# The first FFN of a hybrid transformer layer rewritten in two phases with a seven-product form

## The chip, the cores and the metric

The kernel runs on one core of a Trainium2 chip. The metric is device time in microseconds, from the start to the end of one execution. All arithmetic that matters is float32, which TensorE is fed as pairs of `float32r` tiles: a high part (a cast copy) and a low part (the rest). Each mathematical product term therefore costs three matmuls.

## The reference

One layer over 1024 latent tokens `x` and 256 context tokens `ctx`, model width 1024, FFN width 2816 (22 blocks of 128 columns). Cut to what matters here:

```
mx = modulation(c, ...);  mc = modulation(c_ctx, ...)         # silu(c) @ w_mod, 9 vectors of 1024 each
def pre(h, g, shift, scale):  return rms_norm(h, g) * (1 + scale) + shift
def swiglu(u, wg, wu, wd):    return (silu(u @ wg) * (u @ wu)) @ wd
x   = x   + 0.5 * gate * rms_norm(swiglu(pre(x, ...),   ...))  # first FFN, both streams, same weights
h_c = h_c + 0.5 * gate * rms_norm(swiglu(pre(h_c, ...), ...))
ux, uc = pre(x, ...), pre(h_c, ...)
x = x + post(token_mixer(ux, uc))                              # attention + gated recurrence
x = x + 0.5 * post(swiglu(pre(x)))                             # second FFN, latent tokens only
```

## The kernel before, in words

Tokens stand in three chunks, `CH`: chunks 0 and 1 are 512 latent tokens each, chunk 2 is the 256 context tokens. Activations lie transposed (features on partitions, tokens along the free dimension). `uh[i]`, `ul[i]` hold the high and low part of the scaled input of chunk i. `term` (L102 to L104) issues the three matmuls of one product term, `mm3` a row of terms.

The program is written as straight Python loops for a tile framework. It inserts all waits, gives out buffers of pools (a pool of n buffers makes the n+1st tile wait), and orders each engine's instructions by their place in the program and by `tc.high_priority()` marks. All DMAs of the part at issue are issued from SP's queue. Every weight goes through a staging tile `st` of a pool with three buffers (`stp`, 512 KB each), shared with the modulation weights `w_mod`; ScalarE casts it to the high part (L93) and VectorE subtracts to get the low part (L94), in `load_w`.

The first FFN is the function `ffn`. For a pair of FFN blocks it loads gate, up and down weights, and for each chunk computes gate and up products into PSUM (`gu`, 8 terms each), applies silu and the multiplication, splits the result in high and low part, and goes on at once with the down products (`down`), which VectorE adds into an SBUF accumulator `ys` (L354). So the weights of a block are loaded once for the three chunks, apart from the first block and the last ones. The first block is done chunk by chunk (`block_by_chunk`), the last blocks in an order of chunks that ends with chunk 1 in two halves of 256 tokens, so that its norm can begin early.

`start1` prepares the inputs: sums of squares (`row_norms`), the first two modulation vectors as dot products on VectorE (`mod_first`, L155), and the scaled input (`build_u`) with GpSimd at L457 and L460 and ScalarE at L458 and L459. Modulation vectors 2 to 8 are 56 tasks (`mod_stream`, L155, 512 wide) that are handed out between the products; a task of vectors 2 to 4 has four dot products, one of 5 to 8 has two.

The residual, the two norms and the next input are a generator, `Norms.chain`, advanced by `pump` calls between products. After the first FFN the token mixer begins with key and value projections and filler projections (tiles `qb`, `fb`) of chunks 2 and 0; chunk 1 is needed only after that.

The second FFN, late in the kernel, already has two phases through device memory (`h_d`) and a seven-product form, `winograd`, of gate and up: two FFN blocks of 128 and two chunks of 512 tokens make a 2 by 2 block product, with the 1024 features cut in two halves. Seven products of four terms replace eight. It has no context tokens and no modulation tasks beside it.

Of the kernel before, what the change touches and what calls it, by code (L numbers as in the profile page):

```python
# [19 lines left out]
P = 128  # L20
D = 1024
# [32 lines left out]
def hybrid_block(ctx: ExitStack, tc: tile.TileContext, xT, cc, cols, w_mod, w_gate, w_up, w_down, w_tok, w_col,  # L54
# [26 lines left out]
    f_d = [dram.tile([512, T], F32, name=f"f{i}_d") for i in range(2)]  # L81
    h_d = dram.tile([DFF, SEQ], F32, name="h_d")
# [221 lines left out]
    def ffn(which, chunks, heads, ends, ys, wp, hp, psA, psB, finish, start, pump, tasks=(), before=lambda sub: None):  # L304
        tasks = list(tasks)
        nblk = NF // 2

        slots = [len(tasks), 0, 14 * (nblk - len(ends[0]) - heads[-1][0]) - 4]

        def work():  # L310
            slots[1] += 1
            while slots[0] - len(tasks) < min(slots[0], slots[0] * slots[1] / slots[2]):
                tasks.pop(0)()

        def gu(ws, sub, k_outer=False, pump=None):
            i, c0, n = sub
            cs_ = slice(c0, c0 + n)
            acc = [[psA.tile([P, 512], F32, name="bank")[:, 0:n] for _ in range(2)] for _ in ws]
            if k_outer:
                order = [(j, e, k) for k in range(KT) for j in range(len(ws)) for e in range(2)]  # L320
            else:
                order = [(j, e, k) for j in range(len(ws)) for e in range(2) for k in range(KT)]
            for j, e, k in order:
                w = ws[j][e]
                term(acc[j][e], (w[0][:, k, :], w[1][:, k, :], uh[i][:, k, cs_], ul[i][:, k, cs_]), k == 0, k == KT - 1)
                if k_outer:
                    if j == len(ws) - 1 and e == 1:
                        pump()
                elif k == KT - 1 and pump:
                    for _ in range(n // 256):  # L330
                        pump()
            hs = []
            for pg, pu in acc:
                sl = hp.tile([P, 512], F32, name="sl", bufs=2)[:, 0:n]
                hh, hl = [hp.tile([P, 512], R, name="h")[:, 0:n] if i < 2 else hp.tile([P, 256], R, name="hc", bufs=4)
                          for _ in range(2)]
                with tc.high_priority():
                    act.activation(sl, pg, AF.Silu)
                    dve.tensor_tensor(sl, pu, sl, op=ALU.mult)  # L339
                    act.copy(hh, sl)  # L340
                    dve.tensor_tensor(hl, sl, f32(hh), op=ALU.subtract)
                hs.append((hh, hl))
            return hs

        def down(ws, hs, sub, d, first, urgent=False):
            i, c0, n = sub
            py = psB.tile([P, 512], F32, name="y")[:, 0:n]
            mm3(py, [(w[0][:, d, :], w[1][:, d, :], h[0], h[1]) for w, h in zip(ws, hs)])
            yd = ys[i][:, d, c0:c0 + n]
            with tc.high_priority(None if urgent else 0):  # L350
                if first:
                    act.copy(yd, py)
                else:
                    dve.tensor_tensor(yd, py, yd, op=ALU.add)  # L354

        def gcol(wsrc, f, eng=dve):
            return load_w(wp, wsrc[which, f], KT, eng)

        def row(f):
            return load_w(wp, w_down[which, f], KT)  # L360

        def block(b, todo):
            fs = (2 * b, 2 * b + 1)
            hs = {sub[0]: [] for sub in todo}
            for f in fs:
# [1056 lines left out]
```

## Time and profile before

| | us |
|---|---|
| median of 3 runs | 2764.76 (2763.84 to 2765.48) |
| the profiled execution: its own time | 2770.57 |
| its span | 2768.8 |
| TensorE busy | 2666.1 (96%) |
| VectorE busy | 1713.5 (62%) |
| ScalarE busy | 1091.9 (39%) |
| GpSimd busy | 163.1 (6%) |

The page divides the span into 40 slices of 69.2 us; the first FFN fills the first 15 of them, the second FFN's products and its down phase the last nine or so. A matmul's busy time is modelled, and matmuls overlap, so their cost is read from the distance of their starts, not from their busy time.

### The profile page before, as it was taken

How to read it: one execution, taken by the hardware profiler on the slowest of the kernel's cores; microseconds unless marked ns; L12 is line 12 of the kernel's file. 1: busy time of each engine (PE TensorE's matmuls, PEld its weight loads, DVE VectorE, ACT ScalarE, POOL GpSimd, SP SyncE). 2: the span in 40 equal slices, each digit the busy share in tenths (PEclk: the TensorE clock that was granted, in tenths of full speed). 3: DMA queues.
4: the chain of work that ended last, by engine and by line, in shares of the span. 5: the costliest groups of instructions: out<-in, count | busy, mean ns of one | idle time of the engine just before them, and what ended most of it. 6: DMA issues, size and time to landing. Idle time of an engine off the chain costs nothing.

```text
span 2768.8 us, 37806 instructions
## 1 busy us (share of the span) xinstructions
PE 2666.1 (96%) x14928; PEld 2283.7 (82%) x14928; DVE 1713.5 (62%) x3268; ACT 1091.9 (39%) x1611; POOL 163.1 (6%) x160
## 2 busy tenths in 40 slices
PE   4799999999999989999999999999999999999998
PEld 3588888888888888989998878887887888888897
DVE  7855554354434887566665559944479776664465
ACT  3531111111111444157776676524354433332443
POOL 4610000000000000110000000001100000000000
PEclk9899999999999999999999999999999999999999
DMA  6562223232211343221111144335344322225474
GB/s 226 170 186 77 69 84 106 69 107 69 70 45 62 100 134 125 87 77 37 45 45 51 35 155 130 104 112 186 125 137 136 114 96 88 73 99 181 165 236 156
DMA packets 138129, 302.49 MB, mean 109 GB/s; under 512 B 13920, under 2 KB 53472, under 8 KB 137952
## 3 DMA queue, kind: packets, MB, share of 16 engines
q1 hardware_dynamic: 137952, 300.08, 33.9%
q8 instruction: 117, 1.92, 0.3%
q14 instruction: 60, 0.49, 0.1%
HBM read 248.13 MB, written 51.90 MB: 108 GB/s over the span
## 4 chain that ended last, share of the span: by engine, by line
PE 83%; DVE 8%; ACT 3%; DMA 3%; issue 2%; POOL 0%; SPq 0%; DVEq 0%; ACTq 0%; POOLq 0%
PE bank L103 17%; PE bank L102 17%; PE bank L104 17%; PE y L102 4%; PE y L103 3%; PE y L104 3%; PE fb L103 3%; PE fb L104 3%; PE fb L102 3%; PE S L756 3%; PE bank L772 2%; PE po L785 1%; PE po L786 1%; DMA st<-in_w_down 1%; PE qb L102 1%
## 5 line engine op out<-in xcount | busy, mean ns | idle before, releaser
L102 PE MATMUL bank<-uh,w 128*128 128x512 f32 (+1 forms) x1888 | 682.0, 363 | 23.9 <-ACT uh L459 14.6
L103 PE MATMUL bank<-ul,w 128*128 128x512 f32 (+1 forms) x1888 | 684.6, 363 | 6.6 <-POOL ul L460 6.6
L104 PE MATMUL bank<-uh,w 128*128 128x512 f32 (+1 forms) x1888 | 683.1, 362 | 0.3 <-DVE w L94 0.3
L102 PEld LDWEIGHTS bank<-uh,w 128*128 128x128 f32 x1888 | 358.2, 190 | 80.2 <-ACT uh L459 17.0
L103 PEld LDWEIGHTS bank<-ul,w 128*128 128x128 f32 x1888 | 358.9, 190 | 62.7 <-POOL ul L460 9.7
L104 PEld LDWEIGHTS bank<-uh,w 128*128 128x128 f32 x1888 | 359.4, 190 | 53.3 <-DVE w L94 0.7
L93 ACT CAST w<-st 128x1024 fp32r<-128x1024 f32 x170 | 176.9, 1048 | 457.6 <-PE y L103 250.2
L94 DVE TENSOR_TENSOR w<-st,w 128x1024 fp32r<-128x1024 f32 x164 | 202.1, 1238 | 151.9 <-ACT w L93 143.4
L102 PE MATMUL fb<-uh,w 128*128 128x512 f32 (+1 forms) x576 | 222.1, 386 | 0.3 <-ACT w L93 0.3
L104 PE MATMUL fb<-uh,w 128*128 128x512 f32 (+1 forms) x576 | 220.0, 382 | 0.0
L103 PE MATMUL fb<-ul,w 128*128 128x512 f32 (+1 forms) x576 | 219.1, 380 | 0.0
L354 DVE TENSOR_TENSOR y<-y,y 128x512 f32<-128x512 f32 (+1 forms) x248 | 144.2, 587 | 107.6 <-PE y L104 106.1
L102 PE MATMUL y<-h,w 128*128 128x512 f32 (+1 forms) x368 | 143.3, 391 | 9.3 <-DVE y L354 5.7
L339 DVE TENSOR_TENSOR sl<-bank,sl 128x512 f32<-128x512 f32 (+1 forms) x68 | 39.9, 588 | 179.2 <-PE bank L104 175.0
L103 PE MATMUL y<-h,w 128*128 128x512 f32 (+1 forms) x368 | 142.4, 387 | 0.0
L104 PE MATMUL y<-h,w 128*128 128x512 f32 (+1 forms) x368 | 141.4, 385 | 0.1
L1132 ACT CAST w<-st 128x512 fp32r<-128x512 f32 x126 | 78.1, 621 | 142.2 <-PE bank L104 128.7
L776 DVE TENSOR_TENSOR pl<-bank,ph 128x512 fp32r<-128x512 f32 x160 | 108.2, 684 | 28.2 <-ACT ph L775 28.2
L1133 DVE TENSOR_TENSOR w<-st,w 128x512 fp32r<-128x512 f32 x126 | 86.7, 690 | 62.1 <-ACT w L1132 61.7
L104 PEld LDWEIGHTS fb<-uh,w 128*128 128x128 f32 x576 | 108.3, 188 | 18.6
L102 PEld LDWEIGHTS fb<-uh,w 128*128 128x128 f32 x576 | 108.5, 188 | 18.1 <-ACT w L93 0.5
L103 PEld LDWEIGHTS fb<-ul,w 128*128 128x128 f32 x576 | 108.4, 188 | 17.8
(290 smaller groups left out, 5119.8 us busy)
## 6 DMA issues: line engine op xcount, KB each, us to landing
st<-in_w_down SPq DMA_DIRECT2D x94, 512.0 KB, 3.7
st<-in_w_mod SPq DMA_DIRECT2D x77, 512.0 KB, 3.7
st<-in_w_gate SPq DMA_DIRECT2D x54, 512.0 KB, 3.7
st<-in_w_up SPq DMA_DIRECT2D x54, 512.0 KB, 3.7
st<-in_w_col SPq DMA_DIRECT2D x36, 512.0 KB, 3.7
hst<-h_d SPq DMA_DIRECT2D x22, 512.0 KB, 4.5
h_d<-pc SPq DMA_DIRECT2D x36, 256.0 KB, 2.0
gate_d<-ft SPq DMA_DIRECT2D x32, 256.0 KB, 2.6
```

The source lines that it names most:

```text
L93: act.copy(hi, st)
L94: eng.tensor_tensor(lo, st, f32(hi), op=ALU.subtract)
L102: pe.matmul(ps, lh, rh, start=first, stop=False)
L103: pe.matmul(ps, lh, rl, start=False, stop=False)
L104: pe.matmul(ps, ll, rh, start=False, stop=last)
L339: dve.tensor_tensor(sl, pu, sl, op=ALU.mult)
L354: dve.tensor_tensor(yd, py, yd, op=ALU.add)
L756: pe.matmul(S[:, cs_], qT[:, (s * 2 + t) * P:(s * 2 + t + 1) * P], kT[g][:, cs_], start=(s == 0), stop=(s == 1))
L772: pe.transpose(pt[:, (a * 2 + t) * P:(a * 2 + t + 1) * P], prob[t][:, kt * P:(kt + 1) * P], ident)
L776: dve.tensor_tensor(pl.rearrange("p a q -> p (a q)"), pt, f32(ph).rearrange("p a q -> p (a q)"), op=ALU.subtract)
L1132: act.copy(h, v)
L1133: dve.tensor_tensor(l, v, f32(h), op=ALU.subtract)
```

## The change

The second FFN's seven-product helper is made general (`operands`, `seven`) and used for the first FFN as well. The first FFN becomes two phases. Phase 1 computes gate and up and writes their product to device memory, `h1_d`. The first four blocks go chunk by chunk with plain products (`head1`, which loads the weights anew for each chunk). For the other nine pairs the x tokens go by seven products; the context tokens keep plain products, with the quarters a11, a12, a21, a22 of the same weights, so that eight tiles are split instead of seven (`whole`). Phase 2 reads `h1_d` back and accumulates the 22 down terms of four output blocks in PSUM, for each chunk and each half of the outputs (`half1`), in the order of chunks 0, 2, 1; the down weights are loaded once for each chunk.

In the input scaling, GpSimd's two multiplications and ScalarE's scale are replaced by two fused VectorE operations; the weights of the first block are split on VectorE instead of GpSimd. The context's first two modulation vectors are computed with chunk 2 instead of chunk 1.

```diff
-    def ffn(which, chunks, heads, ends, ys, wp, hp, psA, psB, finish, start, pump, tasks=(), before=lambda sub: None):
...
+    def operands(wp, src, pr, whole):
+        s = []
+        for e in range(2):
+            st = stp.tile([P, 1024], F32, name="st")
+            sp.dma_start(out=st, in_=src[2 * pr + e])
+            s += [st[:, 0:512], st[:, 512:1024]]
+        a11, a12, a21, a22 = s
+        names = ["a11", "a12", "s1", "s2", "s3", "s4", "a21", "a22"] if whole else ["a11", "s1", "s2", "s3", "s4", "a12", "a22"]
+        ws = {k: wp.tile([P, 1024], R, name="w") for k in names}
...
+        sp_("a11", a11)
+        if whole:
+            sp_("a12", a12)
+            sp_("a21", a21)
+        sp_("a22", a22)
+        s1, s3, s2, s4 = a22, a21, a11, a12
+        dve.tensor_tensor(s1, a21, a22, op=ALU.add)
+        sp_("s1", s1)
+        dve.tensor_tensor(s3, a11, a21, op=ALU.subtract)
+        dve.tensor_tensor(s2, s1, a11, op=ALU.subtract)
+        sp_("s2", s2)
+        if not whole:
+            sp_("a12", a12)
+        dve.tensor_tensor(s4, a12, s2, op=ALU.subtract)
+        sp_("s3", s3)
+        sp_("s4", s4)
...
+    def seven(bank, pc, ws, B, post, work=lambda: None, extra=None):
+        def product(w, b):
+            ps = bank()
+            mm3(ps, quarter(ws[w], B[b]))
+            work()
+            return ps
+
+        p1, p5, u2, u3 = (pc.tile([P, 512], F32, name="pc") for _ in range(4))
+        if extra:
+            extra(0, (ws["a11"], ws["a12"]))
+        ps = product("a11", "b11")
+        with tc.high_priority():
+            act.copy(p1, ps)
+        ps = product("s1", "t1")
+        with tc.high_priority():
+            act.copy(p5, ps)
+        add_now(u2, product("s2", "t2"), p1)
+        if extra:
+            add_now(p1, product("a12", "b21"), p1)
+            post(0, 0, p1)
+        add_now(u3, product("s3", "t3"), u2)
+        add_now(u2, u2, p5)
+        add_now(p5, u3, p5)
+        post(1, 1, p5)
+        add_now(u2, product("s4", "b22"), u2)
+        post(0, 1, u2)
+        if extra:
+            extra(1, (ws["a21"], ws["a22"]))
...
+        add_now(u3, product("a22", "t4"), u3)
+        post(1, 0, u3)
...
-                pool.tensor_tensor(u32, ys[i][:, d, :], rows[i], op=ALU.mult)
-                act.activation(u32, u32, AF.Identity, bias=mods[:, 0, d, s:s + 1], scale=gpre[:, 0, d, s:s + 1])
-                act.copy(h, u32)
-                pool.tensor_tensor(ul[i][:, d, :], u32, f32(h), op=ALU.subtract)
+            dve.scalar_tensor_tensor(u32, ys[i][:, d, :], gpre[:, 0, d, s:s + 1], rows[i], op0=ALU.mult, op1=ALU.mult)
+            act.activation(h, u32, AF.Identity, bias=shift)
+            dve.scalar_tensor_tensor(ul[i][:, d, :], u32, shift, f32(h), op0=ALU.add, op1=ALU.subtract)
...
+    start1(0)
+    head1((0, 1), 0, True)
+    start1(1)
+    for f in range(2, 2 * HEAD):
+        head1((f,), 0)
+    start1(2)
+    for f in range(2 * HEAD):
+        head1((f,), 1)
...
+    for k in range(4):
+        t1 = less(parts(1, k), parts(0, k))
+        t2 = less(parts(1, 4 + k), (t1,))
+        t4 = less(parts(0, 4 + k), (t2,))
+        for j, v in enumerate((t1, t2, t4)):
+            split(th[j][:, k], tl[j][:, k], v)
+    for f in range(2 * HEAD):
+        head1((f,), 2)
+    for k in range(4):
+        v = less(parts(1, 4 + k), parts(1, k))
+        split(uh[1][:, k], ul[1][:, k], v)
...
+    ntask, calls, total = len(tasks), [0], 7 * 2 * (NF // 2 - HEAD) - 16
...
+        seven(bank1, pc, operands(w1, w_gate[0], pr, True), B, gate_post, work, ctx_gate)
+        seven(bank1, pc, operands(w1, w_up[0], pr, True), B, up_post, work, ctx_up)
...
+    def load_h1(i, q):
+        o, n = CH[i]
+        st = stp.tile([P, 1024], F32, name="st")[:, 0:2 * n].rearrange("p (a b) -> p a b", a=2)
+        sp.dma_start(out=st, in_=rows_p(h1_d[2 * q * P:(2 * q + 2) * P, o:o + n]))
+        h, l = place(i, q)
+        split(h, l, st)
...
+    def half1(i, g, order, fresh, after=lambda q: None):
+        n = CH[i][1]
+        ps = [bank1()[:, 0:n] for _ in range(4)]
+        for x, q in enumerate(order):
+            if fresh(x):
+                load_h1(i, q)
+            st = stp.tile([P, 1024], F32, name="st").rearrange("p (a b) -> p a b", a=2)
+            sp.dma_start(out=st, in_=w_down[0, 2 * q:2 * q + 2, :, g * 512:(g + 1) * 512].rearrange("f p d -> p f d"))
+            wh, wl = [w1.tile([P, 1024], R, name="w").rearrange("p (a b) -> p a b", a=2) for _ in range(2)]
+            split(wh, wl, st)
+            for d in range(4):
+                cs_ = slice(d * P, (d + 1) * P)
+                for e in range(2):
+                    term(ps[d], (wh[:, e, cs_], wl[:, e, cs_], *hs[q][e]), x + e == 0, x == NF // 2 - 1 and e == 1)
+            after(q)
+            for _ in range(3):
+                nrm.pump()
...
+    for i in (0, 2, 1):
+        half1(i, 0, pairs, lambda x: True)
+        if i == 1:
+            half1(1, 1, pairs[3:] + pairs[:3], lambda x: x >= 8)
+        else:
+            half1(i, 1, pairs, lambda x: False)
+        for c0 in range(0, CH[i][1], 256):
+            nrm.add((i, c0, 256), ys[i], 0, xT, x1T, 1)
```

## Rows read from the trace of the kernel before

**Rows 1.** The page's slices: tenths busy in 40 slices of 69.2 us.

```profile
PE   4799999999999989999999999999999999999998
DVE  7855554354434887566665559944479776664465
DMA  6562223232211343221111144335344322225474
```

**Rows 2.** Stretches: length, then busy us of each engine, PEclk, DMA, GB/s.

```profile
core 0: us, PE busy (x) PEld busy (x) DVE busy (x) ACT busy (x) POOL busy (x), PEclk, DMA share, GB/s
0.00:200.00 200.00, 140.85 (x634) 112.45 (x635) 146.64 (x277) 84.57 (x139) 85.76 (x60) 0.92 0.61 196
200.00:960.00 760.00, 759.90 (x4002) 652.51 (x4001) 374.26 (x754) 130.12 (x194) 0.00 (x0) 1.00 0.25 78
965.00:980.00 15.00, 7.06 (x43) 5.92 (x42) 14.38 (x29) 5.73 (x9) 0.00 (x0) 0.80 0.74 223
980.00:990.00 10.00, 10.00 (x34) 8.14 (x35) 6.27 (x28) 0.00 (x0) 0.00 (x0) 0.62 0.60 190
```

**Rows 3.** PE groups by line and form, first 200 us: busy, mean ns.

```profile
L103 PE MATMUL bank<-ul,w 128*128 128x512 f32 x102 | 45.6, 447 | 6.6 <-POOL ul L460 6.6
...
L103 PE MATMUL bank<-ul,w 128*128 128x256 f32 x48 | 13.5, 281 | 0.0
L102 PE MATMUL y<-h,w 128*128 128x512 f32 x32 | 13.2, 414 | 3.2 <-ACT y L352 1.7 <-ACT w L93 1.5
...
L102 PE MATMUL y<-hc,w 128*128 128x256 f32 x16 | 4.6, 296 | 0.7 <-ACT y L352 0.7
```

**Rows 4.** PE timeline, start and duration: two 512-wide matmuls, two 256-wide ones.

```profile
399.70 0.39 PE L103 MATMUL y<-h,w 128*128 128x512 f32 x1
...
401.96 0.39 PE L104 MATMUL y<-h,w 128*128 128x512 f32 x1
...
2645.07 0.28 PE L102 MATMUL bank<-uh,w 128*128 128x256 f32 x1
...
2647.95 0.28 PE L102 MATMUL bank<-uh,w 128*128 128x256 f32 x1
```

**Rows 5.** Startup timeline: POOL, a DVE operation beside it and alone, first product.

```profile
15.01 6.94 POOL L94 TENSOR_TENSOR w<-st,w 128x1024 fp32r<-128x1024 f32 x3 [13.71 <-ACT w L93]
...
19.71 2.26 DVE L199 TENSOR_TENSOR nw<-nw 128x4 f32<-128x4 f32 x1
...
22.40 0.16 DVE L199 TENSOR_TENSOR nw<-nw 128x4 f32<-128x4 f32 x1
...
33.88 0.80 PE L102 MATMUL bank<-uh,w 128*128 128x512 f32 x1 [8.08 <-ACT uh L459]
```

**Rows 6.** DVE timeline where it is full: start, duration.

```profile
35.11 1.21 DVE L155 SCALAR_TENSOR_TENSOR st<-st,crow 128x1024 f32<-128x1024 f32 x1
...
260.08 0.69 DVE L155 SCALAR_TENSOR_TENSOR st<-st,crow 128x512 f32<-128x512 f32 x1
260.69 0.08 DVE L155 DVE_READ_ACCUMULATOR st<-st,crow 128x1 f32 x1
260.69 0.69 DVE L155 SCALAR_TENSOR_TENSOR st<-st,crow 128x512 f32<-128x512 f32 x1
...
2131.41 0.70 DVE L1143 TENSOR_TENSOR sl<-y,y 128x512 f32<-128x512 f32 x1
2132.02 0.70 DVE L1133 TENSOR_TENSOR tl<-sl,th 128x512 fp32r<-128x512 f32 x1
...
2140.10 2.36 DVE L94 TENSOR_TENSOR w<-st,w 128x1024 fp32r<-128x1024 f32 x2
```

**Rows 7.** Stretches in the second FFN: its products; its down phase, 256 tokens.

```profile
2200.00:2480.00 280.00, 280.00 (x1237) 231.86 (x1236) 195.57 (x296) 95.84 (x162) 0.00 (x0) 1.00 0.27 89
2640.00:2680.00 40.00, 40.00 (x336) 39.99 (x335) 27.87 (x43) 14.32 (x16) 0.00 (x0) 1.00 0.80 258
```

**Rows 8.** The page's DMA issues: count, size, us from issue to landing.

```profile
st<-in_w_mod SPq DMA_DIRECT2D x77, 512.0 KB, 3.7
```

**Rows 9.** DVE groups of the first FFN, modulation tasks: busy, mean ns, idle before.

```profile
L155 DVE SCALAR_TENSOR_TENSOR st<-st,crow 128x512 f32<-128x512 f32 x112 | 73.5, 688 | 26.4 <-DMA st<-in_w_mod 26.3
...
L155 DVE SCALAR_TENSOR_TENSOR sq<-st,crow 128x512 f32<-128x512 f32 x48 | 31.3, 688 | 13.6 <-DMA st<-in_w_mod 13.5
```

**Rows 10.** The stretch behind the first FFN's last matmul.

```profile
1029.00:1080.00 51.00, 50.86 (x359) 47.33 (x358) 45.21 (x146) 23.56 (x47) 2.88 (x8) 1.00 0.46 141
```

More of the change, by code (lines that the diff above doesn't have):

```diff
@@ new lines, in hybrid_block, with stage, next_spare, start1 @@
+    spare = ys[2].rearrange("p a b -> p (a b)").rearrange("p (t d) -> p t d", d=D)
+    turn = [0]
+    def stage():
+        return stp.tile([P, D], F32, name="st")
+    def next_spare():
+        turn[0] += 1
+        return spare[:, turn[0] % 2] if turn[0] % 3 else stage()
+    def start1(i):
+        if i == 0:
+            with tc.high_priority():
+                row_norms(0)
+            def before(d):
+                mod_first(d, 0, next_spare)
+                if d == 4:
+                    fetch(1)
+                if d == 7:
+                    row_norms(1)
+            build_u(0, before)
+            fetch(2)
+            sp.dma_start(out=crow[1], in_=cc[1:2].partition_broadcast(P))
+            act.activation(crow[1], crow[1], AF.Silu)
+        elif i == 1:
+            def before(d):
+                if d == 4:
+                    row_norms(2)
+            build_u(1, before)
+        else:
+            build_u(2, lambda d: mod_first(d, 1, stage))
@@ new lines, in hybrid_block @@
+    sp.dma_start(out=crow[0], in_=cc[0:1].partition_broadcast(P))
+    sp.dma_start(out=col, in_=cols)
+    act.activation(crow[0], crow[0], AF.Silu)
+    fetch(0)
+    start1(0)
[6 more added lines that the diff above has]
+        head1((f,), 1)
+    e_ctx.close()
+    tp = pool_of(p_ctx, "tk1")
+    th = [tp.tile([P, 4, 512], R, name=f"t1h{j}") for j in range(3)]
+    tl = [tp.tile([P, 4, 512], R, name=f"t1l{j}") for j in range(3)]
@@ L417, in hybrid_block @@
+    while tasks:
+        tasks.pop(0)()
+    p_ctx.close()
+    a_ctx.close()
+    np_ = pool_of(n1_ctx, "ffn1n", side="right")
     nrm = Norms(np_, psN, dg='sq')
@@ new lines, in hybrid_block, with place @@
+        ys[i] = pool_of(cm, f"ffn1d{i}", side="right").tile([P, KT, CH[i][1]], F32, name=f"y{i}")
+    sb = pool_of(f1_ctx, "hs1")
+    hsl = [sb.tile([P, 2, 2, 512], R, name=f"hs{j}") for j in range(4)]
+    slots = [(t[:, 0], t[:, 1]) for t in hsl]
+    slots += [(uh[i][:, q:q + 2], ul[i][:, q:q + 2]) for i in (1, 0) for q in range(0, 8, 2)]
+    def place(i, q):
+        if i == 0:
+            return slots[q]
+        if i == 1:
+            return slots[q % 8]
+        h, l = slots[q // 2]
+        c = q % 2 * 256
+        return h[:, :, c:c + 256], l[:, :, c:c + 256]
@@ L1227, in up_post @@
             sp.dma_start(out=h_d[r0:r0 + P, i * 512:(i + 1) * 512], in_=t)
[L1229 to L1230 removed]
+        seven(bank, pc, operands(wp, w_gate[1], pr, False), B, gate_post)
+        seven(bank, pc, operands(wp, w_up[1], pr, False), B, up_post)
     def slot(f):
```

356 lines of the change are left out of this document (127 added, 229 removed).

## The prediction

> **What bounds the kernel now.** I read the page's slices first [rows 1]: TensorE is full from the third slice on, and VectorE's digits in slices 3 to 13, the first FFN, are 3 to 5. So TensorE sets the pace there, and what is gained or lost in the first FFN is a number of matmuls, or time in which TensorE stands. Then I read stretches [rows 2]. From 200 to 960 us TensorE is busy 759.9 of 760 us and VectorE 374. The losses stand at the two ends: in the first 200 us TensorE is busy 141 us, part of it at a lower granted clock (mean 0.92), and between 965 and 980 us it is busy 7 of 15 us, after which the clock is 0.62 for 10 us.
>
> A matmul's cost is the distance of starts [rows 4]: ten 512-wide ones take 2.26 us, so 0.226 each; 24 of the 256-wide ones take 2.88 us, 0.120 each.
>
> How much is lost at the start? The groups of the first 200 us [rows 3], times three lines, are 402 wide and 192 narrow matmuls: 402 x 0.226 + 192 x 0.120 = 114 us of work, so 86 us are lost.
>
> **The matmuls.** Counted from the code, the first FFN has 3024 wide and 1872 narrow matmuls (the last block's chunk 1 runs as halves of 256). Afterwards: plain heads 4 x 2 x 8 x 3 x 2 = 384 wide, products 9 pairs x 2 x 7 x 4 x 3 = 1512, down 1056, together 2952; narrow ones 1056 + 528 = 1584. That is 683.4 + 224.6 = 908.1 us against 667.2 + 190.1 = 857.2 us: **-50.9 us**. No row speaks of another rate: the second FFN's products run at 0.226 with TensorE never idle [rows 7].
>
> **The startup.** GpSimd leaves it. Its operations slow VectorE: L199 on 4 elements takes 2.26 us while GpSimd splits weights and 0.16 us without it [rows 5]. In exchange VectorE takes GpSimd's work, 24 weight splits (the heads load their weights once per chunk), and the operands T1 to T4. Its list up to the first pair, at distances of starts where it is full [rows 6], 0.61 us for 512 and 1.18 for 1024 elements: norms 22 us; 32 dot products of 1.21 with about 0.4 of small operations, 51; fused scaling 27; weight splits 28; gating 6; 56 operations for T1 to T4, 34; first operand set 7. Together 175 us, behind a start at 9 us and some waits that no edit removes: the first pair at about 188 us, as T3 and the last operands may come later than its first product. DMA says nearly the same: x 5.2 MB, w_mod 16.8, weights 12.6, the first pair 2.1, c 1.0, h1 2.6, in all 40.3 MB, takes 206 us at the 196 GB/s of the first 200 us [rows 2] and 156 us at 258 GB/s, the most that a row shows [rows 7]. TensorE's work until then is 384 x 0.226 + 192 x 0.120 = 110 us, so 78 us are lost instead of 86: **-8 us**, with bounds of -31 (165 us) and +10 (206 us). Moving the context's dot products behind chunk 1's scaling costs nothing of its own: chunk 0's and chunk 1's heads, 43 us each, cover them.
>
> **The products.** One pair takes TensorE 168 x 0.226 + 96 x 0.120 = 49.5 us. VectorE has 24 operand operations, 14 sums and 4 gatings of 512, and two of 256: 26 us. The 56 modulation tasks fall on 110 products, 7.1 for a pair; in the first 3.4 pairs a task has four dot products of 0.61 us, 17 us per pair, later two. So VectorE is at 88% for 3.4 pairs and then at 71%. In the second FFN's products it is busy 195.6 of 280 us, 70%, and TensorE does not stand [rows 7]. Only the 3.4 pairs go beyond that; their price lies between 0 and 35 us (the upper end is what waits of 0.7 us for each of the 56 tasks, as now [rows 9], cost when nothing covers them). I take **+8**, nearer to zero, as 70% cost nothing.
>
> By the Trainium skill, "VectorE: DVE Perf Modes", section "The DRAIN you can't avoid", a VectorE operation does not start until the one before has left the pipe. The rows say otherwise: operations of 0.70 us start 0.61 us apart. By that rule the first pairs would take VectorE 42 x 0.69 + 1 + 7.1 x 4 x 0.69 = 50 us, over TensorE's 49.5, and the first rival would gain weight.
>
> **The staging tiles.** They are three, for 4 weight loads and 7.1 task loads per pair. So a tile may be held 3 x 49.5 / 11.1 = 13.4 us on average. A task holds one about 7 us: 3.7 to land [rows 8], 2.4 for four dots, some wait. An operand tile is held longer, since s1 overwrites a22 in place only once a21 and a22 are split, and their two weight buffers come free with the fifth and sixth product of the set before; about 17 us until s4 is split. The mean is (4 x 17 + 7.1 x 7) / 11.1 = 10.6 us: enough, at no cost, with a third of the room left for what I don't see.
>
> **The down phase.** Accumulation in PSUM takes VectorE's additions into `ys` away; nothing waited for them. The wide chunks need two loads of 512 KB in 24 x 0.226 = 5.4 us, 193 GB/s, below what [rows 7] show. Chunk 2 needs more: 11.5 MB of weights, 2.9 MB of h1, and the residual and result of chunk 0's norm, 4.2 MB, in 528 x 0.120 = 63 us, 293 GB/s. At 258 GB/s [rows 7] it takes 72 us. VectorE has 33 us of splits there and about 42 us of chunk 0's norm, part of which may run into chunk 1. I take **+8**, bounds 0 and 25. Handing over between the phases and between halves: 3.7 us to land and about 2.3 us to split, mostly under the last products, as six banks serve four: **+2**, bounds 0 and 5.
>
> By the Trainium skill, "SBUF — State Buffer", section "Summary: rules for kernel authors", one should reckon with about 358 GB/s from HBM. No row here reaches it; by that figure the 18.6 MB take an estimated 52 us, chunk 2 would lose nothing to DMA, and the sum would be 8 us lower.
>
> **The end.** The stall at 965 us, 7.9 us idle and some 5 us at the lower clock [rows 2], came with the norms of chunks 0 and 2; these now run under chunk 1's 120 us of down products: **-13**, bounds -13 and -5. But both halves of chunk 1 now end together, where before one half's norm ran under the other's products. VectorE is already busy 45.2 of the 51 us behind the last matmul [rows 10], in which the mixer computes what does not need chunk 1 (8 fillers and 3 pairs of projections, 50 us). About 11 us of the first half's norm come on top: **+8**, bounds 0 and 25.
>
> **Sum.** -50.9 - 8 + 8 + 2 + 8 - 13 + 8 = -45.9 us. The profiled execution took 2770.6 us (span 2768.8, 1.8 outside it), 5.8 us over the median of the runs; 2770.6 - 45.9 = 2724.7, and by the same distance the median becomes **2719 us**. With all lower ends it would be 2667, with all upper ends 2809.
>
> **Rivals.** *VectorE becomes the bound* in the startup, the first pairs and the mixer's beginning, because distances are nearer 0.69 us and the waits for w_mod are not covered. For: VectorE's list of 175 us is as long as the startup, and 88% is above anything that rows show without loss. Against: [rows 6]. Startup +5 instead of -8, a pair 42 x 0.69 + 1 + 19.6 + 5.0 = 54.6 us and so +17 for 3.4 pairs instead of +8, the end +23 instead of +8: 2756 us, still faster. The skill's rule on the pipe says this one; [rows 6] speak against its reason but not against the waits.
>
> *The staging tiles set the pace, and it gets slower.* One mechanism, in the product stage: loads in the order of the program, tasks ahead of the next set's operands, and operand tiles held until the set is half done. It decides from a mean hold of 13.4 us; at 15.5 us a pair takes 11.1 x 15.5 / 3 = 57 us, and over the 7.9 pairs with tasks that is 62 us, in place of 8: 2773 us. For: the holds above are estimates, an operand tile held 29 us is enough, and no row shows tasks and sets of eight together. Against: tasks need no product and can be drawn ahead, and tasks end 16 products before the phase does.
>
> *The seven products' gain is hidden* is no rival, since TensorE is what bounds this stretch; a sum within 0.2% needs losses of 45 us in other places.
>
> **Chances.** About 0.2%, 5.5 us, is what a measurement of this kernel can tell from no change. As forecast, 2695 to 2745: 0.60. Below that, because the startup is shorter or nothing is lost behind it: 0.07. VectorE as the bound, to 2759: 0.12. Between 2759 and 2770: 0.05. Staging tiles, above: 0.16. So faster 0.79, same 0.05, slower 0.16. The range 2690 to 2775 leaves out some 0.05 below and 0.12 above; the forecast case's own range is 2695 to 2745.
>
> **What would show it.** Right: nine pairs of 49 to 51 us each with TensorE without idle time; first pair's first product near 188 us; GpSimd without work in the startup; the last down product near 975 us instead of 1029; chunk 2's down stretch about 70 us; no more than 10 us of idle TensorE in the mixer's first 60 us. Wrong: TensorE waiting for operand splits in the products, which in turn wait for st (staging) or stand behind dot products (VectorE); a low granted clock in the product stage; a first pair later than 210 us; a stall over 25 us behind chunk 1's last product.

## The result, and the profile after

The changed kernel takes **2726.9 us** (median of four runs, 2725.4 to 2729.2) against 2764.8 us before in the same runs (2763.8 to 2765.5). The ratio is 0.9864, with a 95% interval of 0.9847 to 0.9881: faster by 1.4%, 37.9 us. The forecast was 2719 us, with a range of 2690 to 2775. The profiled execution took 2725.4 us with a span of 2723.6, that is 45.2 us less than the span of before; the forecast difference was 45.9.

So between the two profiled executions the sum came out within a microsecond. Between the medians it is 8.0 us off: the profiled execution of before was 5.8 us above its median, that of after 1.5 us below, and part of the agreement is this accident. The terms of the sum did not come out: one of them is wrong by 38 us, and smaller errors of the other sign make up for it. The runs below are mostly about that one.

First the page's slices of the kernel after, 40 slices of 68.1 us, against [rows 1].

```profile
PE   3799999999979999999999999999999999999998
DVE  8899876765376457566665569844389767664465
PEclk9899999999989999999999999999999999999999
```

TensorE (PE) still sets the pace. VectorE (DVE) has gone from 3 to 5 tenths in the first FFN to between 5 and 9 up to the tenth slice. TensorE has a weak start and one weaker slice, the twelfth (749 to 817 us: a 7, with the clock at 8), which had a 9 in [rows 1]. Stretches of the kernel after, with busy us of each engine, the granted clock (PEclk), DMA share and GB/s:

```profile
core 0: us, PE busy (x) PEld busy (x) DVE busy (x) ACT busy (x) POOL busy (x), PEclk, DMA share, GB/s
0.00:200.00 200.00, 139.41 (x694) 118.53 (x695) 175.70 (x367) 79.93 (x122) 0.70 (x6) 0.97 0.64 214
185.00:630.00 445.00, 445.00 (x2364) 384.98 (x2363) 338.29 (x726) 129.01 (x229) 0.00 (x0) 1.00 0.43 137
759.00:821.00 62.00, 42.32 (x289) 40.99 (x288) 50.72 (x135) 26.98 (x45) 0.00 (x0) 0.80 0.50 156
821.00:856.00 35.00, 35.00 (x277) 34.62 (x277) 20.40 (x19) 18.12 (x20) 0.00 (x0) 0.97 0.73 237
983.00:1050.00 67.00, 64.90 (x450) 59.80 (x450) 51.89 (x174) 26.54 (x54) 3.03 (x8) 1.00 0.39 123
```

Read from top to bottom. In the first 200 us TensorE stands about as long as in [rows 2], 60.6 us against 59.2, though GpSimd (POOL) has left the start; what is better is the clock, 0.97 against 0.92. The nine pairs, 185 to 630 us, have TensorE full at full clock, while VectorE is 76% busy there. The loss is in the third row: chunk 2's first down half, where TensorE is busy 42 of 62 us at a mean clock of 0.80. Its second half, the fourth row, is full. The mixer's beginning, the last row, stands 2.1 of 67 us; in [rows 10] it was 0.14 of 51.

From the starts of the matmuls in the trace, phase 2 begins at 633.0 us. Chunk 0 takes 121.7 us (119.3 us of matmuls at the distances of [rows 4]). Chunk 2 takes 66.4 and 32.7 us for its halves (31.7 each). Chunk 1 takes 70.0 and 59.6 us (59.7 each). The last down product is at 983.5 us.

What held TensorE in chunk 2's first half is in the chain of waits of 740 to 800 us (start, length, what):

```profile
749.79 4.88 DMA st<-h_d
...
755.22 1.06 ACT w L309
756.30 1.24 DVE w L310
757.55 3.39 DMA st<-h_d
...
762.90 1.13 DVE w L310
764.04 0.61 DVE acc L245
764.78 1.84 PE cb L220 x8
```

and in TensorE's waits of 740 to 825 us (line and tile, what it waited for, total, times, longest):

```profile
PE bank L104 <- DVE ul L310: 9.8, 1, 9.8
PE cb L220 <- DVE acc L245: 5.5, 1, 5.5
```

and in those of SP's queue, 755 to 822 us:

```profile
SPq L613 <- DVE ul L310: 18.6, 3, 15.6
SPq L266 <- DVE y L270: 8.4, 5, 2.4
```

Two readings offer themselves. In the chain's first lines a load of `h1` lands, its pair's weights are split, and only then does the next load start: one pair of loads per 7.8 us here (749.8, 757.6), where a pair's matmuls of chunk 2 take 2.9. That looks like too few **staging tiles**. In its last lines and in the waits TensorE stands behind **chunk 0's norm**: 5.5 us at the norm's own matmuls (`cb`, L220, in TensorE's queue ahead of the down products) until VectorE has summed the squares, and 9.8 us for one split (`ul`, L310). SP's queue stood behind the norm as well. Between 778.0 and 791.9 us it issued no load of phase 2: six loads of the norm's residual (`xt`, L266) and the norm's first write stood ahead, and most of these waited for VectorE's norm operations. And from 800.4 to 816.0 us it waited for the same split `ul`, which gives a staging tile back, before it could load the next `w_down` (L613). VectorE's timeline says what stood ahead of that split (start, duration, operation):

```profile
803.01 0.48 DVE L284 SCALAR_TENSOR_TENSOR y<-y,gpre,cb 128x256 f32<-128x256 f32 x1 [0.64 <-PE cb L236]
...
805.05 1.25 DVE L284 SCALAR_TENSOR_TENSOR y<-y,gpre,cb 128x256 f32<-128x256 f32 x3
806.23 1.27 DVE L286 SCALAR_TENSOR_TENSOR ul<-y,mods,uh 128x256 fp32r<-128x256 f32 x3
...
814.50 0.86 DVE L284 SCALAR_TENSOR_TENSOR y<-y,gpre,cb 128x256 f32<-128x256 f32 x2
```

From 803.4 us that is the norm's output, in one run without a gap. What the two longest waits, 5.5 and 9.8 us, did to TensorE and its clock, with an undisturbed stretch for comparison:

```profile
765.00:770.00 5.00, 5.00 (x24) 5.00 (x25) 3.51 (x9) 1.75 (x4) 0.00 (x0) 0.50 0.30 87
780.00:785.00 5.00, 5.00 (x45) 5.00 (x44) 5.00 (x11) 2.43 (x5) 0.00 (x0) 1.00 0.48 124
805.00:810.00 5.00, 0.74 (x4) 0.53 (x4) 5.00 (x14) 3.04 (x7) 0.00 (x0) 0.97 0.00 1
810.00:815.00 5.00, 0.00 (x0) 0.00 (x0) 5.00 (x14) 2.61 (x6) 0.00 (x0) 0.50 0.00 0
815.00:820.00 5.00, 3.51 (x14) 3.22 (x15) 4.03 (x6) 2.64 (x5) 0.00 (x0) 0.50 0.42 127
```

In the second wait TensorE idles about 10 us while VectorE is full and no transfer runs at all. After either wait the granted clock is 0.50, the 1.2 GHz level, for the first matmuls; after the first wait 24 of them start in 5 us in place of 45. By the distances of the starts, the 35 us that this half takes beyond its 31.7 us of products are some 21 us without work, 8 us of products at the lower level and 6 us of the norm's own matmuls.

At the start, TensorE's longest wait of the first 200 us:

```profile
PE bank L103 <- ACT w L94: 38.5, 2, 23.6
```

and the first weight load in SP's timeline, of before and of after:

```profile
3.88 0.91 SPq L90 DMA_DIRECT2D st<-in_w_gate  x1
...
42.04 0.43 SPq L91 DMA_DIRECT2D st<-in_w_gate  x1
```

TensorE waits 38.5 us, in two pieces, for weights. They stand in SP's queue behind `w_mod`: the first weight load is issued at 42.0 us (before, at 3.9), and the first product comes at 47.7 us in place of the 33.9 of [rows 5].

### The profile page after: what moved, and what is told of

It is laid out like the page before. It is cut to its first block, busy times and chain, and to the rows that moved or that the text cites. A ratio compares the mean times of both kernels' runs of the same rounds, so it can differ in the third digit from the quotient of the medians.

```text
span 2723.6 us, 37758 instructions
## 1 busy us (share of the span) xinstructions
PE 2600.9 (95%) x14568; PEld 2236.9 (82%) x14568; DVE 1819.7 (67%) x3456; ACT 1189.1 (44%) x1743; POOL 80.7 (3%) x106
## 4 chain that ended last, share of the span: by engine, by line
PE 82%; DVE 9%; DMA 4%; ACT 3%; issue 2%; POOL 0%; SPq 0%; DVEq 0%; ACTq 0%; POOLq 0%
PE bank L105 20%; PE bank L104 20%; PE bank L103 20%; PE fb L104 3%; PE fb L105 3%; PE fb L103 3%; PE S L884 3%; PE bank L900 2%; DMA st<-h_d 1%; PE po L913 1%; PE po L914 1%; DMA st<-in_w_mod 1%; PE qb L103 1%; PE qb L105 1%; PE qb L104 1%
## 5 line engine op out<-in xcount | busy, mean ns | idle before, releaser
L103 PE MATMUL bank<-uh,w 128*128 128x512 f32 (+1 forms) x1792 | 644.8, 361 | 46.4 <-ACT w L94 38.5
L105 PE MATMUL bank<-uh,w 128*128 128x512 f32 (+1 forms) x1792 | 644.6, 361 | 3.9 <-DVE w L310 3.1
L309 ACT CAST w<-st 128x512 fp32r<-128x512 f32 (+1 forms) x336 | 234.0, 704 | 423.1 <-PE bank L105 165.5
L310 DVE TENSOR_TENSOR w<-st,w 128x512 fp32r<-128x512 f32 (+1 forms) x336 | 264.6, 793 | 177.7 <-ACT w L309 170.0
L95 DVE TENSOR_TENSOR w<-st,w 128x1024 fp32r<-128x1024 f32 x110 | 135.0, 1229 | 82.9 <-ACT w L94 79.4
L94 ACT CAST w<-st 128x1024 fp32r<-128x1024 f32 x110 | 115.2, 1048 | 134.7 <-PE bank L104 51.7
L314 DVE TENSOR_TENSOR pc<-bank,pc 128x512 f32<-128x512 f32 x180 | 123.6, 687 | 59.9 <-PE bank L105 59.5
L156 DVE SCALAR_TENSOR_TENSOR st<-st,crow 128x512 f32<-128x512 f32 (+1 forms) x133 | 99.8, 771 | 57.9 <-DMA st<-in_w_mod 57.8
L887 DVE TENSOR_REDUCE mx<-S 128x1 f32<-128x1280 f32 x64 | 95.4, 1491 | 36.7 <-PE S L884 36.7
L104 PE MATMUL bank<-hs,w 128*128 128x512 f32 (+1 forms) x304 | 107.2, 353 | 1.7 <-DVE hs L310 1.7
L903 ACT CAST ph<-bank 128x512 fp32r<-128x512 f32 x160 | 90.3, 586 | 40.7 <-PE bank L900 39.8
```

The lines of the kernel that those rows point to most:

```text
L94: act.copy(hi, st)
L95: eng.tensor_tensor(lo, st, f32(hi), op=ALU.subtract)
L103: pe.matmul(ps, lh, rh, start=first, stop=False)
L104: pe.matmul(ps, lh, rl, start=False, stop=False)
L105: pe.matmul(ps, ll, rh, start=False, stop=last)
L156: dve.scalar_tensor_tensor(junk, st, 1.0, row, op0=ALU.mult, op1=ALU.mult, accum_out=out)
```

## The experiments

The runs ask four things: was the seven products' saving real and in full on the path; what made chunk 2 slow; was VectorE near to being the bound in the product stage; what bounds the start. Two kernels after them put together what was found. Medians of the kernel before in these series were 2765.5 to 2765.8 us.

**Plain products in two phases.** The operand sets and the third sums are gone, all else stays.

```
-        seven(bank1, pc, operands(w1, w_gate[0], pr, True), B, gate_post, work, ctx_gate)
-        seven(bank1, pc, operands(w1, w_up[0], pr, True), B, up_post, work, ctx_up)
+        for f in (2 * pr, 2 * pr + 1):
+            ws = [load_w(w1, src[0, f], KT) for src in (w_gate, w_up)]
+            for i in (0, 1, 2):
+                acc = [bank1()[:, 0:CH[i][1]] for _ in range(2)]
+                for a, w in zip(acc, ws):
+                    mm3(a, [(w[0][:, k, :], w[1][:, k, :], uh[i][:, k, :], ul[i][:, k, :]) for k in range(KT)])
+                    work()
+                gated(f, i, acc)
```

> Two phases kept, but the nine pairs compute gate and up by plain products for all three chunks (eight terms where the change has seven; the sums T1, T2 and T4 are still made, T3 and the operand sums S1 to S4 are not). If the seven products' saving is on the path in full: nine pairs take 494 us instead of 445, 49 us more than after the change, 2773 to 2779 us, and VectorE's share of them falls. If part of it was hidden by VectorE or staging: less than 40 us more, below 2768 us.

Measured: 2775.2 us, ratio to before 1.0034 (1.0021 to 1.0047); 48.3 us more than the change. A stretch of its product stage:

```profile
300.00:350.00 50.00, 50.00 (x254) 42.74 (x253) 22.07 (x57) 6.43 (x9) 0.00 (x0) 1.00 0.38 119
```

TensorE is as full here as with seven products, and VectorE falls to 44%. So the saving is on the path in full: 48.3 of the 48.8 us counted (216 wide matmuls of 0.226). And the two phases without the products would have been slower than the kernel before, by 0.3%.

**Own staging tiles for h1.**

```
+    h1st = pool_of(f1_ctx, "h1st", 2)
-    hsl = [... for j in range(4)]
+    hsl = [... for j in range(3)]
...
-            return slots[q % 8]
+            return slots[q % 7]
...
-        st = stp.tile([P, 1024], F32, name="st")[:, 0:2 * n]...
+        st = h1st.tile([P, 1024], F32, name="hst")[:, 0:2 * n]...
...
-            half1(1, 1, pairs[3:] + pairs[:3], lambda x: x >= 8)
+            half1(1, 1, pairs[4:] + pairs[:4], lambda x: x >= 7)
```

> Phase 2's h1 tiles are loaded through two staging buffers of their own; w_down keeps the three (to make room, three instead of four h1 slots are fresh, so chunk 1's second half loads four pairs again, not three). Staging theory: chunk 2's first half, 69 us after the change against 32 us of matmuls, is paced by one pair of loads (h1 and w_down) per 6.4 us through three common tiles; with tiles of their own it shrinks to 40 to 55 us, and the run takes 2700 to 2713 us. VectorE theory: chunk 0's norm work stands ahead of the splits; staging changes nothing, 2722 to 2730 us. Bandwidth theory (the DMA engines can't bring a pair of loads in less than 6 us): no change, 2722 to 2730 us.

Measured: 2713.3 us, ratio 0.9810 (0.9795 to 0.9824), 13.6 us less than the change. Chunk 2's two halves:

```profile
762.00:816.00 54.00, 43.31 (x315) 42.19 (x314) 48.11 (x130) 24.03 (x39) 0.00 (x0) 0.87 0.47 151
816.00:847.00 31.00, 31.00 (x260) 31.00 (x259) 21.34 (x21) 19.54 (x22) 0.00 (x0) 1.00 0.83 281
```

The first half takes 53.3 us instead of 66.4, which is the staging theory's number at its upper end. (In the profiles of the runs that leave phase 2 as it is in the change, the half takes 63.5 to 67.4 us.) But TensorE still stands 11 us in it, with VectorE busy for 89% of the time. The second half's loads run at 281 GB/s, above every row of before, so the bandwidth theory is out. Chunk 1's first half falls too, from 70.0 to 63.7 us. Against that, phase 2 begins 7.7 us later (640.6). Nearly 2 us of that are there before the first pair; 5.7 are a wait of TensorE for the first `h1` tile, whose load is issued at 633.1 us, in the change at 618.0: the new tiles lie where the products' tiles were and wait for these.

**Late norms.**

```
...
+    for i in (0, 2):
+        half1(i, 0, pairs, lambda x: True)
+        half1(i, 1, pairs, lambda x: False)
+    norms(0)
+    half1(1, 0, pairs, lambda x: True)
+    norms(2)
+    half1(1, 1, pairs[3:] + pairs[:3], lambda x: x >= 8)
+    norms(1)
```

> Chunk 0's norm is handed out in chunk 1's first half and chunk 2's in chunk 1's second half, so nothing but splits is on VectorE in chunk 2's two halves. VectorE theory: chunk 2 runs at the pace of its matmuls or near it, 30 to 40 us less, 2687 to 2697 us, with up to 10 us given back before the mixer, where chunk 2's norm now ends later. Staging theory: chunk 2's first half stays above 60 us (11 pairs of loads at 6 us and more), and only the idle stretch of about 13 us that stood behind the norm's 24 operations goes, 2710 to 2725 us.

Measured: 2703.5 us, ratio 0.9777 (0.9760 to 0.9793), 23.4 us less than the change. Stretches of 35 us that hold chunk 2's halves, and chunk 1's first half:

```profile
755.00:790.00 35.00, 34.02 (x281) 33.66 (x279) 21.17 (x24) 18.39 (x24) 0.00 (x0) 1.00 0.64 201
790.00:825.00 35.00, 34.34 (x270) 33.65 (x271) 19.57 (x19) 17.05 (x20) 0.00 (x0) 1.00 0.72 228
825.00:890.00 65.00, 61.44 (x292) 50.36 (x291) 56.75 (x136) 32.12 (x47) 0.00 (x0) 1.00 0.63 202
```

By the starts of its matmuls chunk 2's first half takes 31.6 us, its second 33.6. The staging theory's forecast for this run, over 60 us with the common three tiles, fell. Up to 761 us this kernel too issues a pair of loads every 6.3 us; from there to 776 us a `w_down` load comes every 2.6 to 4.1 us and an `h1` load every 3.7 to 4.5. That is slower than the 2.9 us of a pair's matmuls, but six of the eleven `h1` loads are issued before the half begins, and that is enough. As a theory of its own the tiles are out. That own tiles helped all the same has its reason in the trace of the change: a tile can't be given back while its split stands behind the norm, as in SP's wait of 15.6 us above. Late norms take the norm's loads and writes out of SP's queue in chunk 2, too; no run parts this from the time that the norm takes on VectorE. The time lies 6 us above the VectorE theory's range, as chunk 1's halves, now with the norms of chunks 0 and 2 beside them, still take 70.0 and 62.8 us. Nothing was given back in the mixer: TensorE is busy 64.9 of the 67 us behind the last product, as with the change.

**Both.**

```
...
+        st = h1st.tile([P, 1024], F32, name="hst")[:, 0:2 * n]...
...
+    norms(0)
+    half1(1, 0, pairs, lambda x: True)
+    norms(2)
+    half1(1, 1, pairs[4:] + pairs[:4], lambda x: x >= 7)
```

> Own staging tiles and late norms together. If both causes are there: chunk 2's first half at 35 to 45 us, its second half at 32 us, the first FFN's last down product 30 to 45 us earlier than after the change, 2685 to 2700 us. If the DMA engines are the bound: 2715 us and more.

Measured: 2697.4 us, ratio 0.9752 (0.9738 to 0.9767). Chunk 2's halves and chunk 1's first:

```profile
760.00:792.00 32.00, 32.00 (x265) 31.84 (x264) 17.11 (x18) 14.24 (x18) 0.00 (x0) 1.00 0.51 170
792.00:823.00 31.00, 31.00 (x261) 31.00 (x260) 18.10 (x17) 16.24 (x18) 0.00 (x0) 1.00 0.72 241
823.00:889.00 66.00, 66.00 (x321) 55.42 (x320) 57.89 (x139) 34.00 (x49) 0.00 (x0) 1.00 0.66 214
```

No idle time is left in chunk 2. The savings don't add up (13.6 + 23.4 against 29.5), as they must not if the tiles cost only through the norm. Chunk 1's first half is full too: its 66 us are 59.7 of down products and the norm's own matmuls.

**A thin norm.** Chunk 0's norm stays in chunk 2, but its steps are spread.

```
-            for _ in range(3):
+            for _ in range(3 if i != 2 else x % 2):
                 nrm.pump()
```

> Chunk 0's norm stays in chunk 2's two halves, but is handed out at one pump per two pairs, not three per pair, so that its steps spread over both halves. If the bunching is what cost (TensorE stands behind the norm's own matmuls that wait for sums not made yet, and splits behind its 24-operation run): chunk 2's two halves take 68 to 80 us in place of 97, 2704 to 2716 us. If the amount of norm work beside chunk 2's splits is what costs (42 us of norm and some 40 us of splits on VectorE beside 63 us of matmuls): 80 us or more for the two halves, 2712 to 2725 us.

Measured: 2718.9 us, ratio 0.9831 (0.9814 to 0.9849). Chunk 2's halves, and chunk 1's first:

```profile
760.00:795.00 35.00, 35.00 (x295) 35.00 (x295) 25.04 (x55) 18.64 (x25) 0.00 (x0) 1.00 0.65 208
795.00:835.00 40.00, 34.89 (x269) 34.47 (x268) 31.19 (x64) 16.88 (x21) 0.00 (x0) 0.91 0.79 249
835.00:915.00 80.00, 70.45 (x302) 57.41 (x301) 59.94 (x117) 39.42 (x59) 0.00 (x0) 0.91 0.55 180
```

Chunk 2 takes 34.2 + 40.8 = 75.0 us in place of 99.1. That is within the bunching theory's 68 to 80 us, so what cost in chunk 2 is mostly the bunching: three pumps per pair, set for pairs of 5.4 us, ran the whole norm through within a few pairs of 2.9 us. But chunk 1's first half rises from 70.0 to 79.1 us, with the rest of chunk 0's norm and chunk 2's beside its own splits. So 24 us are won and 9 lost in these rows. The whole run wins 8 us, and its time is not in the bunching theory's range (2704 to 2716) but in the other's (2712 to 2725): the amount of norm work counts as well, only in chunk 1. In this profile phase 2 also began 3.4 us later and the part behind the last product took 3.7 us more, neither by an edit of this kernel.

**Denser modulation tasks.**

```
-    ntask, calls, total = len(tasks), [0], 7 * 2 * (NF // 2 - HEAD) - 16
+    ntask, calls, total = len(tasks), [0], 55
```

> The modulation tasks in the product stage are handed out twice as densely (one per product call instead of one per two). Counted from the rows after the change, a task of the first 24 is four dot products of 0.685 + 0.082 us, 3.07 us of VectorE, and the rest of that stage's VectorE work fills half of it; 24 such tasks in 95 us and 46 us of the rest are 120 us of work in 95. If VectorE is the next bound there: TensorE idles 20 to 30 us in the first 100 us of the product stage, which aren't given back, 2745 to 2757 us. If VectorE's lateness is absorbed (nothing on the path waits for a task): under 8 us more, below 2735 us.

Measured: 2754.5 us, ratio 0.9953 (0.9937 to 0.9970), 27.6 us more than the change. The first 200 us of its product stage, and TensorE's waits in the stage:

```profile
185.00:235.00 50.00, 48.63 (x262) 41.61 (x262) 45.49 (x122) 10.19 (x18) 0.00 (x0) 1.00 0.50 159
235.00:285.00 50.00, 36.69 (x178) 31.49 (x177) 45.77 (x123) 11.80 (x21) 0.00 (x0) 0.86 0.53 165
285.00:335.00 50.00, 47.12 (x236) 40.28 (x235) 44.33 (x111) 12.77 (x24) 0.00 (x0) 0.97 0.66 213
335.00:385.00 50.00, 49.68 (x263) 42.80 (x262) 42.64 (x103) 12.08 (x22) 0.00 (x0) 1.00 0.63 206
```

```profile
PE bank L103 <- ACT w L309: 16.7, 4, 8.7
```

ScalarE's longest wait in this run, 185 to 335 us, and the same 150 us in the change:

```profile
ACT w L309 <- DMA st<-in_w_gate: 44.2, 4, 23.9
...
185.00:335.00 150.00, 150.00 (x800) 129.82 (x799) 135.42 (x315) 44.39 (x78) 0.00 (x0) 1.00 0.48 151
```

TensorE stands 18 us in these 200 us. Its wait is for operand splits. VectorE is no busier than after the change, 135.6 us of 150 against 135.4: it does no more in a given time when more is asked of it, and the same share goes with idle time of TensorE here and with none there. The size is the VectorE theory's. The staging tiles take part: TensorE's longest wait, 8.7 us up to 246.5, ends with a cast that waited for the load of the next operands, and SP issued that load at 242.3 us, when a dot product had given its tile back; VectorE had no gap from 228 to 246 us.

**The start's order.** Four weight tiles among the first `w_mod` loads; the context's `w_mod` loads in four parts behind chunk 1's heads.

```
+                if d < 4:
+                    pre.append(load_w(w1, (w_gate, w_up)[d % 2][0, d // 2], KT))
...
-    start1(2)
     for f in range(2 * HEAD):
         head1((f,), 1)
+        start1(2, range(2 * f, 2 * f + 2))
```

> The phase 2 of the change as it is; only SP's order at the start differs: the first block's four weight tiles are issued among w_mod's first loads, not behind all sixteen, and the context's w_mod loads two tiles after each of chunk 1's four heads, not all ahead of the first. Queue theory (TensorE's waits of 23.6 and 14.9 us for weights that stand in SP's queue behind w_mod are on the path): the first pair starts 15 to 30 us earlier, 2697 to 2712 us. Bandwidth theory (the DMA engines moved some 300 GB/s in the first 40 us, so what is brought forward delays something else as much): under 8 us less, 2719 us and more.

Measured: 2720.5 us, ratio 0.9837 (0.9819 to 0.9855), 6.4 us less than the change. TensorE's waits of its first 200 us, and three stretches:

```profile
PE cb L220 <- DVE acc L414: 17.8, 2, 15.0
PE bank L103 <- ACT w L309: 12.5, 1, 12.5
```

```profile
140.00:160.00 20.00, 18.22 (x150) 17.80 (x148) 19.93 (x30) 11.41 (x18) 0.00 (x0) 1.00 0.58 184
160.00:180.00 20.00, 8.76 (x58) 7.74 (x58) 20.00 (x35) 6.57 (x13) 0.00 (x0) 0.85 0.12 40
180.00:200.00 20.00, 16.41 (x66) 13.10 (x67) 19.44 (x45) 5.50 (x10) 0.00 (x0) 0.81 0.30 106
```

The waits for w L94 are gone and products start at 27.1 us instead of 47.7. But only a third of it arrives: TensorE now stands at 160 to 200 us, 12.5 us of it for one operand split, with VectorE busy 59.4 of the 60 us from 140 to 200 and DMA at 12%. Neither of the two theories had that. The number is the bandwidth theory's, but not its reason: where TensorE stands, the transfers run at 40 GB/s.

**The start's order, without the token sums.** T1 to T4 aren't computed.

```
+                    pre.append(load_w(w1, (w_gate, w_up)[d % 2][0, d // 2], KT))
...
-    for k in range(4):
-        t1 = less(parts(1, k), parts(0, k))
...
-        v = less(parts(1, 4 + k), parts(1, k))
-        split(uh[1][:, k], ul[1][:, k], v)
-         "t1": (th[0], tl[0]), "t2": (th[1], tl[1]), "t4": (th[2], tl[2])}
+         "t1": (uh[1][:, 0:4], ul[1][:, 0:4]), "t2": (uh[1][:, 4:8], ul[1][:, 4:8]), "t4": (uh[0][:, 4:8], ul[0][:, 4:8])}
```

> The start order with early weights, and the token sums T1 to T4 left out: the products read chunks 0 and 1 themselves where they should read the sums (the number of matmuls is the same, the values are not the reference's). That takes 56 operations of some 0.60 us start distance, 34 us, from VectorE between 138 and 187 us, where it had no gap. VectorE theory (the start order's earlier TensorE waits in 140 to 200 us for splits that stand behind the sums): the 15 us of idle there go, 2702 to 2710 us. Loads theory (w_gate and w_up arrive too late): under 4 us less, 2716 us and more.

Measured: 2700.6 us, ratio 0.9765 (0.9750 to 0.9779), 19.9 us less than with the sums. TensorE is full:

```profile
160.00:180.00 20.00, 20.00 (x104) 17.15 (x104) 17.93 (x47) 5.10 (x9) 0.00 (x0) 1.00 0.53 165
180.00:200.00 20.00, 20.00 (x106) 17.22 (x105) 19.64 (x52) 7.78 (x14) 0.00 (x0) 1.00 0.53 164
```

That is 5 us more than the idle time that the VectorE theory counted. So with early weights it is VectorE's list, with the sums in it, that decides when the pairs can run.

**The change without the token sums.** The same edit on the changed kernel itself.

```
-    for k in range(4):
-        t1 = less(parts(1, k), parts(0, k))
...
+         "t1": (uh[1][:, 0:4], ul[1][:, 0:4]), "t2": (uh[1][:, 4:8], ul[1][:, 4:8]), "t4": (uh[0][:, 4:8], ul[0][:, 4:8])}
```

> The change with the token sums T1 to T4 left out in the same way and nothing else. After the change TensorE had no gap from 120 us on although VectorE was busy for 96% of 130 to 180 us. If the sums are hidden, as the forecast had it: within 3 us of the change, 2724 to 2730 us. If they held back the first pairs: 5 to 15 us less.

Measured: 2729.7 us, ratio 0.9873 (0.9857 to 0.9890), no faster than the change. In the change the sums are hidden: by the loads that come late. The two runs together show two limits of nearly the same height at the start, the order of SP's queue and VectorE's list.

**Staggered norms, and all that was found together.** The two parts of chunk 0's norm six pairs apart, the own staging tiles for chunks 2 and 1 only:

```
+    norm(0, 0)
+    half1(1, 0, pairs, lambda x: True, lambda q: norm(0, 256) if q == 5 else None)
+    norm(2, 0)
+    half1(1, 1, pairs[4:] + pairs[:4], lambda x: x >= 7)
...
+        st = (h1st.tile([P, 1024], F32, name="hst") if i else stp.tile([P, 1024], F32, name="st"))[:, 0:2 * n]...
```

> Late norms as before, the two parts of chunk 0's norm now handed out six pairs apart, and own staging tiles only for the h1 loads of chunks 2 and 1 (chunk 0's go through the common three, since tiles laid where the products' tiles were had to wait for them: 7 us more idle at the hand-over). Expected against the run with both: 5 to 7 us at the hand-over and 2 to 4 us in chunk 1's first half, 2686 to 2693 us; if hand-over idle just moves to the second pair, 2695 to 2699 us.

Measured: 2693.2 us, ratio 0.9736 (0.9720 to 0.9751). Phase 2 begins at 635.2 us, 2.7 us earlier than in the run with both; chunk 1's first half takes 67.2 us and not less than the 65.7 there, so the stagger brought nothing. The last kernel is this one with the start's order:

```
+    norm(0, 0)
+    half1(1, 0, pairs, lambda x: True, lambda q: norm(0, 256) if q == 5 else None)
...
+                    pre.append(load_w(w1, (w_gate, w_up)[d % 2][0, d // 2], KT))
...
+        start1(2, range(2 * f, 2 * f + 2))
```

> The staggered late norms with own staging tiles for chunks 2 and 1, and the start order with early weights, in one kernel. If the two savings are in different places and add up: 2693 less the 6 us of the start order, 2684 to 2690 us. If the start order's earlier TensorE only meets the same wait later: 2691 to 2695 us.

Measured: **2685.6 us**, ratio 0.9711 (0.9696 to 0.9725): 2.9% faster than before, 41.3 us faster than the change. The two savings are in different places and add up.

## Why the forecast was right, and where it was wrong

**The matmuls, -50.9 us: right.** The count and the distances held, and plain products give 48.3 of the counted 48.8 us back.

**The startup, -8 us: right in size, wrong in its mechanism.** The first s1 x t1 product is at 190.5 us; one product of 2.7 us and 24 narrow matmuls of 2.9 us stand ahead of it, so the first pair starts at 185 us (forecast 188), and 75 us are lost in place of 86. The forecast made VectorE's list of 175 us the limit. In the change it is not: without 34 us of that list nothing is faster. TensorE waited for weights in SP's queue instead, a queue that the forecast summed in bytes (156 to 206 us) and did not follow in its order. The list becomes the limit, with 20 us, once the weights come early.

**The products, +8 us: nearly nothing.** From 185 us to the beginning of phase 2 at 633.0 are 448 us against 9 x 49.5 = 446, and the trace lists no wait of TensorE between 190 and 635 us. The staging tiles cost nothing here, as the forecast had it. How large the reserve is no run shows: twice the density of tasks costs 27.6 us, but by the forecast's prices that is an estimated 61 us of VectorE's work in a pair of 49.5, and no run lies between. The rivals' premise (VectorE and the tiles as what binds next in the first pairs) was sound, and their condition was not met. What speaks against the first rival's other premise, distances of 0.69 us, is again VectorE's timeline: three operations of 256 elements take 1.25 us together where one alone takes 0.48. By the Trainium skill, "VectorE: DVE Perf Modes", section "The DRAIN you can't avoid", an operation waits until the one before has left the pipe, which by three times 0.48 would be an estimated 1.44 us; the same section leaves out operations that nothing holds, and these rows are of that kind. The forecast gave the rule without this exception.

**The down phase, +8 and +2 us for handing over: the step that failed.** It lost 48.4 us: 2.4 in chunk 0, 35.7 in chunk 2, 10.3 in chunk 1's first half. The forecast saw the ingredients (33 us of splits, 42 us of norm in 63 us of TensorE) but took bytes as the limit, 72 us at 258 GB/s, and expected the two to mix evenly. They did not. The pumps deal the norm out per pair, and a pair of chunk 2 is half as long, so the norm ran as a block; TensorE, whose queue held the norm's matmuls ahead of the products, stood, the splits stood behind VectorE's runs, and the loads behind the norm's own in SP's queue and behind tiles that the splits had not given back. The parts of that are shown apart: spreading the norm in place takes chunk 2 from 99.1 to 75.0 us, moving it away to 65.2 us, tiles of their own besides to 63.3 us (part of which comes back in chunk 1). Bytes were no limit: the run with own tiles moves 281 GB/s, the run with both has no idle time at 170 and 241, and the change itself moves 334 GB/s at the start.

```profile
20.00:40.00 20.00, 2.08 (x8) 1.78 (x8) 19.93 (x49) 7.73 (x12) 0.00 (x0) 1.00 0.92 334
```

The 358 GB/s from HBM that the Trainium skill gives in "SBUF — State Buffer", section "Summary: rules for kernel authors", are not reached over these 20 us either; over a shorter stretch they are passed, with 404 from 30 to 35 us (roughly measured, as the DMA share there is 1.04). Of the forecast's two figures for bytes, 258 and 358, the skill's lies nearer to both.

**The end: one term too small, one not there.** Before, 21 us were lost between 960 us and the last product at 1028.8 (forecast 13), counted as the time less the matmuls left. From the last product to the end both kernels take 1740 us, so both halves of chunk 1 ending together cost nothing (forecast +8): TensorE stands 2.1 us in the mixer's first 67, as its fillers and projections cover the first half's norm.

**What the forecast missed on the good side.** Up to the last product before lost 1028.8 - 908.1 = 120.7 us and after 983.5 - 857.2 = 126.3, so +5.6, and the mixer lost nothing more, where the forecast's terms without the matmuls sum to +5. With 86 at the start and 21 at the end some 13.5 us were lost before between 200 and 960 us, although TensorE shows 759.9 of 760 us busy there [rows 2]; the forecast put that stretch at nothing. The starts of the matmuls separate it: 4.3 us are the norms' own matmuls, 6.0 us distances among the old down products that are longer than 0.226 or 0.120, and 3.1 us the same among gate and up products. The agreement of the sums is chance: +38 us in the down phase were paid by -6 in the products, -8 at the end, -8 in the mixer, -3 at the start and these -13.5. (The forecast's lower ends sum to 2670 us, not to 2667; nothing hangs on it.)

## What to carry to other kernels

Work that is dealt out by steps of a loop (so many pumps per pair) must be dealt out again when a step's length changes: the same norm that costs 10 us under pairs of 5.4 us (late norms) cost 36 us under pairs of 2.9 us, because the queues of TensorE, VectorE and SP all kept the order they were given. A chain that shows one load after the other in a few tiles isn't yet proof that tiles are missing; look at what the split that frees a tile stands behind. And where loads of a new kind are put at the head of a queue, follow the queue in its order and not in bytes: the first consumer of what stands behind them is where the time goes, until the engine that is nearly as full takes its place.

## What the runs showed of the hardware

- In the product stage VectorE is busy about 135 us of 150 with the tasks as the change deals them out, and no more when they come twice as densely. In the first case TensorE has no wait, in the second it stands 18 us in 200, so the share alone does not tell the two apart.
- After TensorE had stood for 5.5 us, and again after about 10 us with next to no work, its granted clock was 0.50, the 1.2 GHz level, in the next rows (765 to 770 and 815 to 820 us), where 256-wide matmuls start 0.21 us apart in place of 0.12. So these waits cost more than their own length.
